# The second MLP in two passes: chunk 0 by plain products, chunks 1 and 2 together by seven block products

## The chip, the cores and the metric

The kernel runs as one program on one core of a Trainium2 chip. The metric is the device time of one execution in microseconds (us). A core has a matrix engine (TensorE: PE for its matmuls, PEld for the weight loads that run beside them), three engines for elementwise work (VectorE: DVE; ScalarE: ACT; GpSimd: POOL), and SyncE (SP), whose queue issues the transfers here. Every engine works through its own queue in order; an instruction that waits for a semaphore holds up all that stands behind it on that engine. Matmuls write to PSUM banks; everything else named here lies in SBUF or, for the inputs and outputs, in DRAM.

## The reference

The reference computes one step of a two-layer network on 1152 tokens (1024 latent, 128 context) of width 1024. Layer 0 is windowed attention and an MLP, layer 1 is a bidirectional state-space scan with a gated linear unit (GLU) and an MLP; then a final norm. The change concerns the MLP of layer 1 alone:

```
def _mlp(h, w1, w2):                 # h: tokens x 1024, w1: 1024 x 4096, w2: 4096 x 1024
    a = jax.nn.relu(h @ w1)
    return (a * a) @ w2
...
x = x + gate * _mlp(modulate(rmsnorm(x), shift, scale), w1, w2)
y = rmsnorm(x, final_norm_g)
```

## The kernel before

The 1152 tokens lie with the features on the partitions, as three chunks of 384 tokens: `x[0]`, `x[1]`, `x[2]`, each of 8 feature tiles of 128 (KT). Chunk 2 holds 256 latent and 128 context tokens, which have different modulation, so elementwise work on it is done in two pieces, 256 and 128 wide. Each float32 operand of a matmul is split into a high part (a rounded copy) and a low part (the rest), and each product takes three matmuls, `mm3`: high with high, high with low, low with high (L45 to L47). A split of a weight tile is one cast on ACT (L51) and one subtraction on DVE (L52), and it reads a raw tile that a DMA of 512 KB has filled.

`mlp(layer)` runs for both layers. It goes over 16 feature blocks `fb` of 256 hidden features. For each block there is a **first product** (for each chunk and each half m of the block: 8 x 3 matmuls of 384 columns into one PSUM bank, then relu and square on ACT and a split into `at`), and a **second product** (for each chunk and each of 8 output tiles: 2 x 3 matmuls, then `add_x`, which adds the gated bank to `x` on DVE). A block is thus 3 x 48 matmuls of the first product and then 3 x 48 of the second, 288 in all, and the MLP 16 x 288 = 4608.

What the steps of the prediction touch:

- `load` makes the weights of a block, w1 or w2: two raw halves of 128 x 1024, and of each a high and a low part. The raw tiles (`wr`, tag `wr`) have two buffers for everything, so the transfer of a raw half can be issued only when the subtraction that reads the half two places before it is done. The split w1 (tag `wq`, one buffer for the high part, one for the low) and the split w2 (tag `w2`, the same) exist once each: w1 of the next block can be written only when the first product of this block has ended, and w2 only when its second product has ended.
- In the block's code w2 is loaded ahead of the first product, and w1 of the next block between the first and the second product.
- `norm_stats` makes the row statistics of a chunk (`rb`), `norm_apply` the modulated input `mh`. In the second MLP `mh` of chunk 0 is there from the GLU, those of chunks 1 and 2 are made at the start.
- In the last block each chunk's second product is followed by `norm_stats` and `final`, which scales `x` and writes `y`.

The order of the work on each engine is set by a scheduler: the code is recorded in program order, and instructions whose inputs and buffers would be ready are moved up.

## Time and profile before

| | us |
|---|---|
| median of 3 runs (2797.89 to 2807.26) | 2802.87 |
| the profiled execution | 2799.74 |
| its span, first to last instruction | 2797.8 |
| second MLP, from its first matmul (1955.58) to the end of the span | 842.2 |
| PE busy / DVE busy / ACT busy / POOL busy in the span | 2609.5 / 1824.4 / 1096.1 / 366.6 |

The page gives busy time of each engine, then the span in 40 slices of 70 us (a digit is a share in tenths; PEclk is the clock granted to TensorE, in tenths of 2.4 GHz). Matmuls overlap in the pipeline, so their listed duration (0.34 us) is longer than the distance between their starts; where it matters the starts are compared. In the timeline a row gives start, duration, engine, line, operation, tiles, and in brackets the idle time before it and what ended it; rows of a kind that follow each other are merged with their count.

### The profile page before, as it was taken

Reading aid. Unit: us, or ns where it says so; the run is one execution under the profiler, and the core shown is the slowest. Engines: PE = TensorE matmul, PEld = TensorE weight load, DVE = VectorE, ACT = ScalarE, POOL = GpSimd, SP = SyncE. Lnnn points to the kernel's source line nnn. Section 1 sums busy time; section 2 is a strip of 40 time slices with the busy share of each in tenths; the row PEclk is TensorE's granted clock in tenths of the full one; section 3 lists DMA queues with packets and bytes.
Section 4 is the critical chain, followed back from the end, with each engine's and each line's share of the span. In section 5 each row is a group of like instructions: output and inputs, shape, how many; then the busy total and the mean of one; then the engine's idle time right before and its main releaser. Section 6 shows DMA issues by size and latency. Waiting matters only on the chain. (4 is left out here: it accounts for less than half of the span.)

```text
span 2797.8 us, 44016 instructions
## 1 busy us (share of the span) xinstructions
PE 2609.5 (93%) x16561; PEld 2462.1 (88%) x16561; DVE 1824.4 (65%) x4342; ACT 1096.1 (39%) x2295; POOL 366.6 (13%) x476
## 2 busy tenths in 40 slices
PE   6889999998899999999899687999999999999997
PEld 4767987886699989899899676999999999999997
DVE  4847777785576787887875799545645354454455
ACT  3545666662223323332333655434422222212224
POOL 1222222210022132121220400000000000000002
PEclk8999999999999999999999799999999999999998
DMA  7353222235532233132223586433110111111101
GB/s 264 109 169 105 84 79 74 81 116 189 180 103 75 70 95 90 55 105 71 88 83 91 174 251 180 141 121 113 46 46 31 46 46 46 34 43 46 46 31 68
DMA packets 128452, 271.67 MB, mean 97 GB/s; under 512 B 13296, under 2 KB 67952, under 8 KB 126832
## 3 DMA queue, kind: packets, MB, share of 16 engines
q1 hardware_dynamic: 128240, 268.86, 30.3%
q8 instruction: 131, 2.15, 0.3%
q14 instruction: 81, 0.66, 0.1%
HBM read 214.22 MB, written 39.81 MB: 91 GB/s over the span
## 5 line engine op out<-in xcount | busy, mean ns | idle before, releaser
L455 DVE SCALAR_TENSOR_TENSOR x<-m,mod,x 128x384 f32<-128x384 f32 (+2 forms) x1024 | 496.2, 512 | 149.2 <-PE m L47 145.3
L47 PE MATMUL m<-at,w 128*128 128x384 f32 x1536 | 523.4, 341 | 0.0
L45 PE MATMUL m<-at,w 128*128 128x384 f32 x1536 | 522.7, 340 | 0.8 <-DVE x L455 0.8
L46 PE MATMUL m<-at,w 128*128 128x384 f32 x1536 | 521.7, 340 | 0.0
L45 PE MATMUL m<-mh,w 128*128 128x384 f32 x1024 | 349.1, 342 | 1.9 <-ACT mh L237 1.9
L47 PE MATMUL m<-mh,w 128*128 128x384 f32 x1024 | 349.9, 342 | 0.0
L46 PE MATMUL m<-mh,w 128*128 128x384 f32 x1024 | 349.8, 342 | 0.0
L52 DVE TENSOR_TENSOR at<-r,at 128x384 fp32r<-128x384 f32 x192 | 111.6, 583 | 361.4 <-ACT at L51 361.2
L51 ACT CAST w<-wr 128x1024 fp32r<-128x1024 f32 x128 | 131.0, 1046 | 524.4 <-PE m L46 515.7
L47 PEld LDWEIGHTS m<-at,w 128*128 128x128 f32 x1536 | 289.1, 188 | 9.2 <-issue 8.9
L45 PEld LDWEIGHTS m<-at,w 128*128 128x128 f32 x1536 | 289.2, 188 | 3.8 <-issue 1.8
L46 PEld LDWEIGHTS m<-at,w 128*128 128x128 f32 x1536 | 289.1, 188 | 2.8 <-issue 2.5
L683 ACT ACTIVATE r<-m 128x384 f32<-128x384 f32 x192 | 93.8, 490 | 373.1 <-PE m L47 370.3
L45 PEld LDWEIGHTS m<-mh,w 128*128 128x128 f32 x1024 | 193.9, 190 | 7.4 <-issue 4.8
L52 DVE TENSOR_TENSOR w<-wr,w 128x1024 fp32r<-128x1024 f32 x128 | 156.6, 1243 | 64.9 <-ACT w L51 60.6
L47 PEld LDWEIGHTS m<-mh,w 128*128 128x128 f32 x1024 | 194.5, 190 | 3.6 <-issue 3.5
L46 PEld LDWEIGHTS m<-mh,w 128*128 128x128 f32 x1024 | 194.4, 190 | 1.6 <-issue 0.8
L45 PE MATMUL m<-h,w 128*128 128x384 f32 x512 | 174.4, 341 | 1.5 <-ACT w L51 0.7
L47 PE MATMUL m<-h,w 128*128 128x384 f32 x512 | 173.9, 340 | 1.2 <-DVE w L52 1.2
L46 PE MATMUL m<-h,w 128*128 128x384 f32 x512 | 174.5, 341 | 0.0
L1242 POOL TENSOR_TENSOR fo<-fo,rb 128x384 f32<-128x384 f32 x18 | 20.6, 1176 | 1034.7 <-ACT rb L224 1026.9
L389 POOL TENSOR_SCALAR pt<-pt,sst 128x512 f32<-128x512 f32 (+1 forms) x144 | 102.6, 724 | 298.4 <-DVE sst L387 153.8
(328 smaller groups left out, 5161.1 us busy)
## 6 DMA issues: line engine op xcount, KB each, us to landing
wr<-in_w_dram SPq DMA_DIRECT2D x128, 512.0 KB, 4.4
wm<-in_w_mod_dram SPq DMA_DIRECT2D x80, 512.0 KB, 4.6
wr<-in_glu_dram SPq DMA_DIRECT2D x48, 512.0 KB, 3.3
wr<-in_w_qo_dram SPq DMA_DIRECT2D x24, 512.0 KB, 3.3
wr<-in_w_qo_dram SPq DMA_DIRECT2D x48, 256.0 KB, 2.8
bt<-bt_d SPq DMA_DIRECT2D x16, 768.0 KB, 5.5
dt_d<-d SPq DMA_DIRECT2D x32, 294.0 KB, 2.1
D<-dt_d SPq DMA_DIRECT2D x16, 588.0 KB, 4.7
```

The source lines that it names most:

```text
L45: mm(out, lh, rh, start=first, stop=False)
L46: mm(out, lh, rl, start=False, stop=False)
L47: mm(out, ll, rh, start=False, stop=last)
L51: (ceng.copy if ceng is self.nc.scalar else ceng.tensor_copy)(h, src)
L52: seng.tensor_tensor(out=l, in0=src, in1=h, op=ALU.subtract)
L389: nc.gpsimd.tensor_scalar(p[:, e, :nk], p[:, e, :nk], rc[:, e:e + 1], 1.0, op0=ALU.mult, op1=ALU.mult)
L455: nc.vector.scalar_tensor_tensor(out=self.x[c][:, m, lo:hi], in0=ps[:, lo:hi], scalar=self.gate(layer, j, m, s), in1=self.x[c][:, m, lo:hi ...
L683: nc.scalar.activation(r, pt[:, :CW], AF.Relu)
L1242: nc.gpsimd.tensor_tensor(out=z, in0=z, in1=self.rb[c], op=ALU.mult)
```

## The change

`run` calls a new function `mlp1` for the second MLP; `mlp` stays for the first one.

**Pass A, chunk 0.** 16 blocks, first product 48 matmuls, second product 48. The first product of block fb + 1 stands ahead of the second product of block fb. w2 of block fb and w1 of block fb + 1 are loaded ahead of both. Beside it `h_seven` makes five combinations of the inputs of chunks 1 and 2 (sums on POOL, splits on ACT and DVE).

**Pass B, chunks 1 and 2.** 16 blocks again, so w1 and w2 are read a second time. The first product takes the 256 features as two halves of 128, the 1024 inputs as two halves of 512 and the two chunks as a 2 x 2 block product, in Winograd's form of Strassen's algorithm: seven products (`seven`) of 4 x 3 = 12 matmuls, 84 in place of 8 x 12 = 96. They accumulate in three banks `pa`, `pb`, `pc`; after a product a bank's partial sum is copied out (`keep`) or added to a kept one (`done`), then relu, square and split as before. The weights enter as seven tiles, some of them sums of quarters (`w_seven`: 4 sums and 7 subtractions on DVE, 7 casts on ACT, each 128 x 512); for the next block they are made during the second product, and `issue_after` keeps them behind the last square and split in the queues. `h_rest` makes the two inputs that are no sums, at the end of pass A. The second product is as before, 96 matmuls. `final0` writes chunk 0's output in blocks 1 and 2 of pass B, through one buffer `z`.

```diff
+    def w_half(self, fb, q, raw=None):
+        raw = self.R.tile([128, 1024], F32, name="wr", tag="wr", bufs=2)
+        self.nc.sync.dma_start(raw, self.a["w1"][1, fb][:, 1024 * q:1024 * q + 1024])
+        return raw.rearrange("p (k m c) -> p m k c", m=2, c=128)
+    def w_seven(self, fb, w, first=False):
+        nc, M, R = self.nc, self.M, self.R
+        r0, r1 = self.w_half(fb, 0), self.w_half(fb, 1)
+        a11, a21, a12, a22 = r0[:, 0], r0[:, 1], r1[:, 0], r1[:, 1]
...
+        def put(i, src, t):
+            nc.scalar.copy(t[:, 0], src)
+            nc.vector.tensor_tensor(out=t[:, 1], in0=src, in1=t[:, 0], op=ALU.subtract)
+            w[i] = t
+        def sx(x, y, op):
+            t = M.tile([128, 4, 128], F32, name="sx", tag="sx", bufs=2)
+            nc.vector.tensor_tensor(out=t, in0=x, in1=y, op=op)
+            return t
+        def single():
+            put(7, sx(a11, a21, ALU.subtract), one(R, "wo", 2))
+            yield
+            put(2, a12, one(R, "wo", 2))
+            yield
+            put(4, a22, one(M, "wz", 1))
+            yield
+        yield
+        if first:
+            yield from single()
+        t1, t5 = two("ws", "wq")
+        put(1, a11, t1)
+        yield
+        s1 = sx(a21, a22, ALU.add)
+        put(5, s1, t5)
+        yield
+        s2 = sx(s1, a11, ALU.subtract)
+        t6, t3 = two("ws", "wq")
+        put(6, s2, t6)
+        yield
+        put(3, sx(a12, s2, ALU.subtract), t3)
+        yield
+        if not first:
+            yield from single()
+    def seven(self, w, B, pa, pb, pc, evict):
+        for i in (1, 5, 6, 3, 7, 2, 4):
+            p = pa if i in (1, 6, 7, 4) else pb if i in (5, 3) else pc
+            for j in range(4):
...
+                for k, (x, y) in enumerate(((0, 0), (0, 1), (1, 0))):
+                    self.nc.tensor.matmul(p[:, :CW], w[i][:, x, j, :], B[i][j][y], start=f and k == 0,
+                                          stop=j == 3 and k == 2, skip_group_check=True)
...
+            evict(i)
+    def h_seven(self, B):
...
+        for j in range(4):
...
+            c, d = (M.tile([128, CW], F32, name="cd", tag="sx", bufs=2) for _ in range(2))
+            put = lambda i, src: self.split(B[i][j][0], B[i][j][1], src, nc.scalar, nc.vector)
+            self.h_part(1, j, a)
+            self.h_part(2, j, b)
+            yield
+            put(1, a)
+            gp.tensor_tensor(out=a, in0=b, in1=a, op=ALU.subtract)
+            put(5, a)
+            yield
+            self.h_part(2, j + 4, c)
+            self.h_part(1, j + 4, d)
+            yield
+            gp.tensor_tensor(out=b, in0=c, in1=b, op=ALU.subtract)
+            put(7, b)
+            yield
+            gp.tensor_tensor(out=c, in0=c, in1=a, op=ALU.subtract)
+            put(6, c)
+            gp.tensor_tensor(out=d, in0=d, in1=c, op=ALU.subtract)
+            put(4, d)
+            yield
+    def h_rest(self, B):
...
+    def mlp1(self):
...
+            def load(name, pool, tag, src):
+                w = [pool.tile([128, 2048], F32R, name=name, tag=tag, bufs=2) for _ in range(2)]
+                for q in range(2):
+                    sl = slice(1024 * q, 1024 * q + 1024)
+                    raw = self.R.tile([128, 1024], F32, name="wr", tag="wr", bufs=2)
+                    nc.sync.dma_start(raw, src[:, sl])
+                    self.split(w[0][:, sl], w[1][:, sl], raw, nc.scalar, nc.vector)
+                return w
...
+            def act(z, src):
+                at = M.tile([128, 2, CW], F32R, name="at", tag="at", bufs=4)
+                nc.scalar.activation(z, src, AF.Relu)
+                nc.scalar.activation(z, z, AF.Square)
+                self.last = (nc.scalar.copy(at[:, 0], z),
+                             nc.vector.tensor_tensor(out=at[:, 1], in0=z, in1=at[:, 0], op=ALU.subtract))
+                return at
...
+            w1 = load("w1", self.R, "wq", a["w1"][1, 0])
+            h = self.mh[0]
+            def fill():
+                yield from self.norm_stats(2)
+                yield from self.h_seven(B)
...
+            def first(w):
...
+            acts = first(w1)
+            for fb in range(nb):
+                w2 = load("w2", M, "w2", a["w2"][1, fb])
+                if fb + 1 < nb:
+                    w1 = load("w1", self.R, "wq", a["w1"][1, fb + 1])
+                    nxt = first(w1)
+                    next(gen, None)
+                    second(0, w2, acts)
+                    next(gen, None)
+                    acts = nxt
+                else:
+                    for _ in gen:
+                        pass
+                    ws = {}
+                    rest = self.h_rest(B)
+                    sums = self.w_seven(0, ws, True)
+                    def step(m):
+                        next(sums, None)
+                        next(rest, None)
+                    second(0, w2, acts, step)
+                    for _ in chain(sums, rest):
+                        pass
+            out = chain(self.norm_stats(0, 2), self.final0())
+            for fb in range(nb):
+                w2 = load("w2", M, "w2", a["w2"][1, fb])
+                pa, pb, pc = (ps.tile([128, 512], F32, name="m1", tag="acc") for _ in range(3))
...
+                def keep(i, p):
+                    z[i] = self.tt("r")
+                    nc.scalar.copy(z[i], p[:, :CW])
+                def done(o, i, p):
+                    nc.vector.tensor_tensor(out=z[i], in0=z[i], in1=p[:, :CW], op=ALU.add)
+                    at[o] = act(z[i], z[i])
...
+                self.seven(ws, B, pa, pb, pc, evict)
+                last = fb == nb - 1
+                wn = {}
+                sums = iter(()) if last else self.w_seven(fb + 1, wn)
+                sa, va = (i.ins for i in self.last)
+                def part():
+                    with tc.issue_after(sa), tc.issue_after(va):
+                        next(sums, None)
+                part()
+                for c in (2, 1):
+                    stats = self.norm_stats(c, 1) if last else iter(())
+                    def step(m):
+                        next(stats, None)
+                        part()
+                        if m % 2 and fb:
+                            next(out, None)
+                    second(c, w2, [at[0, c], at[1, c]], step)
+                    for _ in stats:
+                        pass
+                    if last:
+                        out = self.final(c, c == 1)
+                ws = wn
             for _ in out:
                 pass
-            for _ in gen:
-                pass
+    def final0(self):
+        nc = self.nc
+        for kt in range(KT):
+            z = self.M.tile([128, CW], F32, name="z", tag="z", bufs=1)
+            nc.scalar.activation(z, self.x[0][:, kt, :], AF.Copy, scale=self.gn[:, 4, kt:kt + 1])
+            nc.gpsimd.tensor_tensor(out=z, in0=z, in1=self.rb[0], op=ALU.mult)
+            nc.sync.dma_start(self.o["y"][0, :, kt], z)
+            yield
...
-        self.mlp(1)
+        self.mlp1()
```

Three places in the order of the built program. A number behind a name tells buffers of one name apart; `h_19343` is the input of chunk 0, `w1` and `w2` are split weights, `wr` raw halves, `m1` and `m2` the banks of the first and second product. Rows of the changed kernel have its own line numbers.

**PE, end of one block of the first loop and start of the next.** Before, the last matmuls of a block's second product and the first of the next block's first product:

```order
L45 MATMUL m2_21289<-at_21027,w2_20895 128x384
L46 MATMUL m2_21289<-at_21027,w2_20895 128x384
L47 MATMUL m2_21289<-at_21027,w2_20896 128x384
L45 MATMUL m1_21309<-h_19343,w1_21088 128x384
L46 MATMUL m1_21309<-h_19343,w1_21088 128x384
L47 MATMUL m1_21309<-h_19343,w1_21089 128x384
```

Now, in pass A, the end of block 11's second product and the start of block 13's first:

```order
L45 MATMUL m2_21944<-at_21713,w2_21798 128x384
L46 MATMUL m2_21944<-at_21713,w2_21798 128x384
L47 MATMUL m2_21944<-at_21713,w2_21799 128x384
L45 MATMUL m1_21975<-h_19343,w1_21965 128x384
L46 MATMUL m1_21975<-h_19343,w1_21965 128x384
L45 MATMUL m1_22006<-h_19343,w1_21965 128x384
L47 MATMUL m1_21975<-h_19343,w1_21966 128x384
```

The first product still follows the second directly, with three matmuls on the high part of w1 (`w1_21965`) moved ahead of the first on its low part (`w1_21966`).

**ACT, around the same place.** Before, from the last half of a block into the next (`L51 CAST` is the high part of a split):

```order
L51 CAST w1_20685<-wr_20687 128x1024
L683 ACTIVATE r_20680<-m1_20655 128x384
L51 CAST w1_20685<-wr_20691 128x1024
L684 ACTIVATE r_20680<-r_20680 128x384
L51 CAST at_20624<-r_20680 128x384
L51 CAST w2_20895<-wr_20897 128x1024
L51 CAST w2_20895<-wr_20901 128x1024
L683 ACTIVATE r_20931<-m1_20906 128x384
```

Now, the same block of pass A as above:

```order
L51 CAST hs11_20514<-cd_21720 128x384
L51 CAST w2_21955<-wr_21957 128x1024
L51 CAST w2_21955<-wr_21961 128x1024
L51 CAST w1_21965<-wr_21967 128x1024
L51 CAST w1_21965<-wr_21971 128x1024
L861 ACTIVATE r_22000<-m1_21975 128x384
```

The casts of w1 moved from the middle of the block before, ahead of the casts of w2, to right behind the casts of w2 of the same turn; on DVE the four subtractions stand in the same sequence, and on SP the transfers of `wr_21967` and `wr_21971` stand behind those of `wr_21957` and `wr_21961`.

**DVE, the second product of a block.** Before, chunk 2 (`x2`, two pieces a tile; `L455` is `add_x`):

```order
L455 SCALAR_TENSOR_TENSOR x2_72<-m2_21244,mod1_94,x2_72 128x256
L455 SCALAR_TENSOR_TENSOR x2_72<-m2_21244,mod1_94,x2_72 128x128
L455 SCALAR_TENSOR_TENSOR x2_72<-m2_21253,mod1_94,x2_72 128x256
L455 SCALAR_TENSOR_TENSOR x2_72<-m2_21253,mod1_94,x2_72 128x128
L455 SCALAR_TENSOR_TENSOR x2_72<-m2_21262,mod1_94,x2_72 128x256
L455 SCALAR_TENSOR_TENSOR x2_72<-m2_21262,mod1_94,x2_72 128x128
```

Now, pass B, a block in the middle (`ws` the seven weight tiles, `sx` sums of quarters):

```order
L455 SCALAR_TENSOR_TENSOR x2_72<-m2_24249,mod1_94,x2_72 128x256
L455 SCALAR_TENSOR_TENSOR x2_72<-m2_24249,mod1_94,x2_72 128x128
L726 TENSOR_TENSOR ws_24233<-sx_24245,ws_24233 128x512
L731 TENSOR_TENSOR sx_24258<-sx_24245,wr_24220 128x512
L455 SCALAR_TENSOR_TENSOR x2_72<-m2_24263,mod1_94,x2_72 128x256
L455 SCALAR_TENSOR_TENSOR x2_72<-m2_24263,mod1_94,x2_72 128x128
L726 TENSOR_TENSOR ws_24260<-sx_24258,ws_24260 128x512
L731 TENSOR_TENSOR sx_24272<-wr_24222,sx_24258 128x512
L455 SCALAR_TENSOR_TENSOR x2_72<-m2_24276,mod1_94,x2_72 128x256
```

Between the additions of chunk 2's eight tiles the eleven instructions on the next block's weights are now queued.

## Rows read from the trace of the kernel before

**Rows 1.** The page: busy time of the engines, and granted clock by slice.
```profile
PE 2609.5 (93%) x16561; PEld 2462.1 (88%) x16561; DVE 1824.4 (65%) x4342; ACT 1096.1 (39%) x2295; POOL 366.6 (13%) x476
PEclk8999999999999999999999799999999999999998
```
**Rows 2.** Second MLP by stage: us; busy PE, PEld, DVE, ACT, POOL; PEclk; DMA share; GB/s.
```profile
1955.58:1981.50 25.92, 23.43 (x128) 22.66 (x129) 21.66 (x52) 14.74 (x30) 0.00 (x0) 0.93 0.13 42
1981.50:2748.00 766.50, 766.50 (x4356) 766.03 (x4355) 357.14 (x652) 203.56 (x354) 0.00 (x0) 1.00 0.12 41
```
**Rows 3.** Timeline, where one block of the second MLP gives way to the next.
```profile
2114.48 0.34 PE L45 MATMUL m<-h,w 128*128 128x384 f32 x1
2114.50 2.00 ACT L51 CAST w<-wr 128x1024 fp32r<-128x1024 f32 x2 [21.99 <-PE m L46]
...
2115.59 2.36 DVE L52 TENSOR_TENSOR w<-wr,w 128x1024 fp32r<-128x1024 f32 x2 [0.16 <-ACT w L51]
...
2116.84 1.46 SPq L658 DMA_DIRECT2D wr<-in_w_dram  x2
```
**Rows 4.** Timeline, PE at the start of the second MLP.
```profile
1974.99 0.51 PE L223 MATMUL nrb<-ident,nst 128*128 128x128 f32 x3 [0.57 <-DVE nst L220]
1977.42 0.79 PE L45 MATMUL m<-mh,w 128*128 128x384 f32 x2 [1.92 <-ACT mh L237]
...
1980.64 0.52 PE L46 MATMUL m<-mh,w 128*128 128x384 f32 x1
```
**Rows 5.** DMA issues of that place: first, second; then all of L658 (to landing).
```profile
wr<-in_w_dram SPq DMA_DIRECT2D x1, 512.0 KB, 3.8
...
wr<-in_w_dram SPq DMA_DIRECT2D x1, 512.0 KB, 5.4
...
DMA to landing us min/median/max: 3.6/4.5/5.4
```
**Rows 6.** Timeline, SP and ACT: a cast of w1 that waits for its transfer.
```profile
1940.74 0.33 SPq L658 DMA_DIRECT2D wr<-in_w_dram  x1
...
1944.47 1.05 ACT L51 CAST w<-wr 128x1024 fp32r<-128x1024 f32 x1 [2.35 <-DMA wr<-in_w_dram]
```
**Rows 7.** Groups by form, second MLP: DVE, then POOL (count, busy us, mean ns).
```profile
L455 DVE SCALAR_TENSOR_TENSOR x<-m,mod,x 128x384 f32<-128x384 f32 x256 | 152.9, 615 | 68.6 <-PE m L47 68.4
L52 DVE TENSOR_TENSOR w<-wr,w 128x1024 fp32r<-128x1024 f32 x62 | 74.4, 1221 | 43.7 <-ACT w L51 43.6
L455 DVE SCALAR_TENSOR_TENSOR x<-m,mod,x 128x256 f32<-128x256 f32 x128 | 61.9, 483 | 40.3 <-PE m L47 40.2
L52 DVE TENSOR_TENSOR at<-r,at 128x384 fp32r<-128x384 f32 x96 | 53.3, 557 | 260.2 <-ACT at L51 260.2
L455 DVE SCALAR_TENSOR_TENSOR x<-m,mod,x 128x128 f32<-128x128 f32 x128 | 43.7, 342 | 0.0
...
L1242 POOL TENSOR_TENSOR fo<-fo,rb 128x384 f32<-128x384 f32 x18 | 20.6, 1176 | 1034.7 <-ACT rb L224 1026.9 <-ACT fo L1241 4.3 <-issue 3.5
```
**Rows 8.** Timeline, PE in the GLU: matmuls right behind a wait and later.
```profile
1755.57 0.78 PE L45 MATMUL gp<-ys,gw 128*128 128x384 f32 x2 [3.49 <-ACT ys L51]
...
1758.57 0.52 PE L46 MATMUL gp<-ys,gw 128*128 128x384 f32 x1
1758.89 0.52 PE L47 MATMUL gp<-ys,gw 128*128 128x384 f32 x1
...
1759.42 0.34 PE L46 MATMUL gp<-ys,gw 128*128 128x384 f32 x1
```
**Rows 9.** Windows behind another wait, in the first MLP (columns as in rows 2).
```profile
1176.00:1178.00 2.00, 1.02 (x17) 0.67 (x17) 1.94 (x11) 0.00 (x0) 0.00 (x0) 0.50 0.11 33
...
1182.00:1184.00 2.00, 2.00 (x12) 2.00 (x11) 2.00 (x5) 0.24 (x1) 1.29 (x2) 0.90 0.39 131
```
**Rows 10.** Group by form, whole kernel, DVE: a subtraction 512 wide.
```profile
L52 DVE TENSOR_TENSOR wo<-wr,wo 128x512 fp32r<-128x512 f32 x48 | 34.5, 720 | 6.9 <-ACT wo L51 6.6
```
**Rows 11.** Issues of the outputs in the last 47 us (KB each, us to landing).
```profile
out_y_dram<-fo SPq DMA_DIRECT2D x12, 384.0 KB, 2.3
```

More of the change, by code (lines that the diff above doesn't have):

```diff
@@ L698, in mlp @@
                         next(stats, None)
-                        if m % 2:
-                            next(out, None)
                     fill(1)
@@ L703, in mlp, with two, one @@
                         pass
-                    if fb == nb - 1 and layer == 1:
-                        out = self.final(c)
+            for _ in gen:
[8 more added lines that the diff above has]
+        a11, a21, a12, a22 = r0[:, 0], r0[:, 1], r1[:, 0], r1[:, 1]
+        def two(name, tag):
+            t = R.tile([128, 2, 2, 4, 128], F32R, name=name, tag=tag, bufs=2)
+            return t[:, 0], t[:, 1]
+        def one(pool, tag, bufs):
+            return pool.tile([128, 2, 4, 128], F32R, name="ws", tag=tag, bufs=bufs)
+        def put(i, src, t):
[30 more added lines that the diff above has]
+            yield from single()
@@ new lines, in h_part @@
+    def h_part(self, c, kt, out):
+        nc = self.nc
+        t = self.tt("nt")
+        for lo, hi, s in self.pieces(c):
+            nc.vector.scalar_tensor_tensor(out=t[:, lo:hi], in0=self.x[c][:, kt, lo:hi],
+                                           scalar=self.gs[1][1][:, kt, s:s + 1],
+                                           in1=self.rb[c][:, lo:hi], op0=ALU.mult, op1=ALU.mult)
+            nc.scalar.activation(out[:, lo:hi], t[:, lo:hi], AF.Identity, bias=self.shift(1, 1, kt, s))
```

88 lines of the change are left out of this document (83 added, 5 removed).

## The prediction

> **What bounds the kernel now.** I read the page first: PE is busy 93% of the span and the granted clock is near full in nearly every slice [rows 1]. Then the stage that the change touches, by windows: from 1981.5 to 2748 PE is busy for all of 766.5 us, at a granted clock of 1.00 (2.4 GHz), and starts 4356 matmuls, so one takes 766.5 / 4356 = 0.176 us and none waits [rows 2]. DVE is busy 47% there, ACT 27%, the DMA engines 12%. So in this stage time is the count of matmuls times 0.176 us, as long as PE never waits. Last I read one place, the change from one block to the next [rows 3]. The cast of the new w2 waits 22 us for the old one's last matmul and begins at 2114.50; the first subtraction follows at 2115.59; the transfer of the next raw half is issued at 2116.84. PE doesn't notice: at 2114.48 it goes on with a first product of 144 matmuls (25.3 us) whose weights were ready. The single buffers of w1, w2 and two raw halves cost nothing because 144 matmuls cover each refill. That is what to see: the chain exists, and its cover is long.
>
> **What is saved.** Pass B has 84 + 96 matmuls a block, pass A 48 + 48, together 276 where 288 were: 16 x 12 = 192 fewer, and 192 x 0.176 = **-33.8 us**. The start of the second MLP loses its wait for chunk 2's input: 0.57 and 1.92 us of idle, then some ten matmuls at about 0.32 us instead of 0.176 (until past 1980.64), 1.4 us [rows 4]: **-3.9 us**. The statistics on PE stay, elsewhere.
>
> **What pass A adds.** Now the first product of one block stands directly behind the second product of another, and it needs a w1 that can't be there. In the order on ACT, DVE and SP, w2's split and then w1's transfers and split are queued in this place. Both raw buffers hold w2's halves until DVE has subtracted them, and w2's split waits for PE's last matmul. So PE itself starts the chain on which it then waits. By the same chain before, with PE's next matmul due at 2114.48:
>
> - ACT casts w2's first half, DVE subtracts it, SP issues w1's first half at 2116.84: 2.36 us [rows 3].
> - The transfer lands 3.8 us after issue, as the first of a pair did here; the second took 5.4, and the extremes are 3.6 and 5.4 [rows 5].
> - ACT casts w1's half: 1.05 us, and it starts as soon as the data lands (issue 1940.74, cast 1944.47, 3.73 apart) [rows 6].
>
> 2.36 + 3.8 + 0.03 + 1.05 and a few hundredths to PE are 7.3 us of idle. Then three matmuls can run on the high part; the low part needs 1.22 us of DVE [rows 7] from the cast's end, so PE goes on at 8.5 us having done 0.5 us of work: 8.0 us lost.
>
> The clock comes on top. In the GLU a wait of 3.49 us was followed by matmuls whose starts are 0.32 us apart (1758.57, 1758.89), the clock of 1.2 GHz, until about 1759.2, 3.7 us after PE went on [rows 8]. Behind a 7.3 us wait I expect the same. From 8.5 to 11.0 us that makes 8 matmuls where 14 would run: another 1.1 us. If the clock stayed full, w1's second half would bind instead (issued 1.13 us later, 5.4 to land, then cast and subtraction: 11.1 us), for about 0.5 us. So a turn costs 8.5 to 9.1 us, and I take **9.1**. If half clock lasts 6 us, as behind the wait that ended near 1176.5 (0.50, and still 0.90 at 1182 to 1184) [rows 9], it is 10.2.
>
> There are 14 such turns: the first products of blocks 2 to 15. 14 x 9.1 = **+127.4 us** (8.3 to 10.2 each: 116 to 143). Block 1's first product waits only for cast and subtraction, since its transfer can land during block 0's; and the last second product waits for one cast of w2: together **+2.4**.
>
> By the Trainium skill (DMA: Bandwidth & Descriptors, Anatomy of one DMA) a transfer costs about 2.0 us fixed plus its bytes at 436 GB/s, an estimate of 3.2 us for 512 KB, and the turns together would cost 8 us less. The trace has 3.6 to 3.8, and I keep that. The Trainium skill's first page (Trainium Kernel Development and Optimization, Best Practices) asks for double buffers so that transfers overlap compute; it speaks against pass A, but it would blame the kernel before as well, where the trace shows no wait at all.
>
> **Beside PE in pass A.** `h_seven` adds 16 sums to POOL at 1.18 us [rows 7] and 44 half-microsecond instructions each to DVE and ACT, spread over ten turns of 26 us in which DVE has 4 x 1.22 + 8 x 0.62 + 2 x 0.56 = 11 us of other work [rows 7]. They stand in the second product, ahead of the chain, and end before it: nothing. The 64 more transfers of 512 KB find the DMA engines at 12%: nothing outside the turns.
>
> **From A to B.** The last second product (8.4 us) and the first products of pass B lie beside DVE's work on `h_rest` (16 x 0.41 + 8 x 0.62 = 11.5), 11 subtractions and sums 512 wide at 0.72 [rows 10] (7.9), 8 additions (4.9) and w2 (2.4): 26.7, or some 24 if queued instructions overlap by 0.08 each (two of 1.22 take 2.36 [rows 3]). PE needs the last of it for its fifth product, after about 8.4 + 60 x 0.176 = 19 us, and starts 1 us late behind a cast: **+6** (2 to 12).
>
> **Pass B.** ACT is at 13 of 32 us a block. DVE: PE's 84 first matmuls end at 14.8 us of a block and the first tile of the second product at 15.9; from there DVE has 8 x (0.483 + 0.342) for chunk 2, 11 x 0.72 for the weights and one split, 15.1 us. Six banks rotate, so chunk 1's sixth tile, due at 28.5 us, needs chunk 2's last addition. At listed durations that is done at 31.0; with the overlap at 28.7. Lost a block: 0 to 2.5 us. The queue is dense, so I stay near the overlap, with a little for subtractions that wait for a cast: 0.6, and 15 x 0.6 = **+9** (0 to 37). `issue_after` holds the sums behind the last split, on which nothing of PE's next 40 matmuls waits. `final0`'s eight tiles go through one buffer: cast 0.6, POOL 1.18 and a transfer of half the 384 KB that land in 2.3 [rows 11] make 4 us against 2.1 of spacing, and ACT's queue stands meanwhile: **+4** (0 to 16). The tail is as before.
>
> **Sum:** -33.8 - 3.9 + 127.4 + 2.4 + 6 + 9 + 4 = +111.1. On the profiled execution's 2799.74 that is 2910.8, so **2911 us**. The median of before is 2802.87, 3.1 higher, less than its runs differ; I leave the number.
>
> **Rivals.**
>
> - *Faster: pass A's turns cost PE nothing.* The point is (33.8 + 3.9 - 2.4 - 6 - 9 - 4) / 14 = 1.2 us a turn; below it the change gains, and with no wait at all the time is 2911 - 127 = 2784. It would need PE to run other matmuls in the turn. For it: PE's order does move three matmuls up. Against: these three read w1's high part, and all else behind them is behind that wait. 0.03.
> - *Only the transfer is hidden* (w1's raw halves in time): w2's two casts, then w1's, 3.2 us, and the low part, some 3.9 a turn: 2838. Against: both raw buffers are full at that point. 0.03.
> - *DVE binds pass B* at listed durations: 2.5 in place of 0.6 a block, +28: 2939. For it: 11 more instructions in a queue that PE's banks wait on. Against: the overlap in [rows 3]. 0.14.
> - *Half clock lasts longer*, 10.2 a turn: 2926. For it: [rows 9]. Against: [rows 4, 8]. 0.12.
> - *Shorter turns*: full clock, or 3.6 us to land: 8.3 a turn, 2900. 0.08.
> - That the products aren't fewer is out: 84 stand in the order.
>
> **How the numbers follow.** The forecast has 0.60. Lowest sum with the turns in place: -37.7 + 116 + 2 + 2 = +82, 2882. Highest: turns of 10.2 and pass B at its worst, the rest as taken: -37.7 + 143 + 2.4 + 6 + 37 + 4 = +155, 2955. The range is 2880 to 2955; outside it lie the first two rivals. A measurement of this kernel tells about 0.3% (8 us) from no change. Faster by more: 0.03, the first rival; within: 0.02, some way between the first two; slower: 0.95.
>
> **What would show it.** In pass A: 14 gaps of about 7 us on PE, ended by a cast of w1 which itself waited for its transfer; granted clock 0.5 behind each; a turn of some 26 us for 96 matmuls, where 16.9 would do. In pass B: PE busy throughout, 180 matmuls in about 32 us. I am wrong if PE's gaps in pass A are under 2 us, or if pass B takes over 34 us a block.

## The result, and the profile after

The changed kernel takes 2918.98 us (median of 4 runs, 2914.43 to 2921.07), the one before 2802.48 us beside it (4 runs, 2797.89 to 2807.26): a ratio of 1.0412, 95% interval 1.0397 to 1.0426, so 116 us slower. The forecast was 2911, its range 2880 to 2955. The profiled execution took 2914.43 us with a span of 2912.6, 114.8 us more than the span of before.

The head of the page after, which answers to [rows 1]. The columns and slices are as there.

```profile
PE 2615.3 (90%) x16369; PEld 2446.5 (84%) x16369; DVE 1994.9 (68%) x4618; ACT 1231.9 (42%) x2519; POOL 384.2 (13%) x492
...
PE   6889999988899999999996879997777889999997
PEclk8999999999999999999998999998888899999998
```

PE is busy 6 us longer than before and the span is 115 us longer: PE does fewer matmuls, does some of them at half clock, and stands idle. The slices show where: from the 28th to the 32nd, 1966 to 2330 us, PE is busy 7 or 8 tenths and the clock is at 8. That is pass A; the slices of pass B behind it are at 9 up to the tail.

Then the waits of PE through the whole second MLP: who waited, for whom, us in total, times, longest.

```profile
PE m L45 <- ACT w L51: 97.6, 16, 7.5
PE m L45 <- DVE x L455: 8.4, 17, 1.2
PE nrb L223 <- DVE nst L220: 3.3, 1, 3.3
PE m L769 <- DVE ws L726: 1.4, 1, 1.4
```

One line carries nearly all of it: 16 waits for a cast of a split weight, 97.6 us, 13 of them 6.9 to 7.5 us long. One of them, as the timeline shows it (the answer to [rows 3], where the same chain stood beside a first product of 144 matmuls):

```profile
2114.28 0.34 PE L47 MATMUL m<-at,w 128*128 128x384 f32 x1
2114.48 1.99 ACT L51 CAST w<-wr 128x1024 fp32r<-128x1024 f32 x2 [2.85 <-PE m L46]
...
2115.55 2.36 DVE L52 TENSOR_TENSOR w<-wr,w 128x1024 fp32r<-128x1024 f32 x2 [0.28 <-ACT w L51]
2116.80 6.63 SPq L854 DMA_DIRECT2D wr<-in_w_dram  x3
2120.77 1.04 ACT L51 CAST w<-wr 128x1024 fp32r<-128x1024 f32 x1 [4.31 <-DMA wr<-in_w_dram]
...
2121.87 0.69 PE L45 MATMUL m<-h,w 128*128 128x384 f32 x1 [7.25 <-ACT w L51]
...
2122.35 0.52 PE L46 MATMUL m<-h,w 128*128 128x384 f32 x1
...
2122.67 0.52 PE L45 MATMUL m<-h,w 128*128 128x384 f32 x1
...
2123.13 0.69 PE L47 MATMUL m<-h,w 128*128 128x384 f32 x1
2123.27 1.04 ACT L51 CAST w<-wr 128x1024 fp32r<-128x1024 f32 x1 [1.45 <-DMA wr<-in_w_dram]
```

PE's last matmul of the second product starts at 2114.28. ACT casts w2, which that product has just released (2114.48), DVE subtracts it (2115.55), SP issues w1's transfer (2116.80, 2.32 us after the cast began), the data lands and ACT casts it (2120.77, 3.97 later), PE goes on (2121.87, 1.10 later). The bracket on PE's row gives 7.25 us of idle. After it the starts are 0.32 us apart, and the low part comes at 2123.13.

The clock around it, and the stages, by windows (length, busy time and count of PE, PEld, DVE, ACT, POOL, then the granted clock and DMA): first the wait, what follows it, and the rest of this turn; then all 14 turns; then pass B's block 0, blocks 1 and 2, blocks 3 to 14, and block 15.

```profile
2114.62:2121.87 7.25, 0.00 (x0) 0.00 (x1) 3.00 (x4) 2.89 (x3) 0.00 (x0) 0.85 0.40 136
2121.87:2126.18 4.31, 4.31 (x13) 3.87 (x14) 2.43 (x2) 1.04 (x1) 0.00 (x0) 0.50 0.39 138
2126.18:2141.13 14.95, 14.95 (x85) 14.63 (x84) 7.84 (x15) 5.85 (x13) 3.24 (x3) 0.99 0.11 36
1981.18:2358.61 377.43, 278.45 (x1360) 268.13 (x1359) 175.45 (x260) 122.98 (x197) 17.07 (x16) 0.82 0.23 78
2368.01:2405.48 37.47, 33.71 (x182) 30.86 (x181) 33.03 (x63) 17.25 (x32) 0.00 (x0) 1.00 0.24 85
2405.48:2474.38 68.90, 65.97 (x377) 64.10 (x376) 49.55 (x100) 34.27 (x65) 8.29 (x7) 1.00 0.24 78
2474.38:2861.18 386.80, 382.03 (x2162) 375.47 (x2161) 270.08 (x529) 163.45 (x289) 1.03 (x1) 1.00 0.20 67
2861.18:2894.27 33.09, 33.09 (x196) 32.79 (x195) 21.41 (x48) 21.12 (x41) 1.32 (x2) 1.00 0.00 1
```

Behind the wait PE has a clock of 0.50 for 4.31 us, then 0.99. The 14 turns take 377.43 us, 26.96 each, of which 96 matmuls at 0.176 are 16.9: **10.06 us a turn are lost, 140.9 in all**. Blocks 3 to 14 take 386.80 / 12 = 32.23 us.

### The profile page after: what moved, and what is told of

Same layout as the page of the kernel before. It is cut to its first block, busy times and chain, and to the rows that moved or that the text cites. A ratio compares the mean times of both kernels' runs of the same rounds, so it can differ in the third digit from the quotient of the medians.

```text
span 2912.6 us, 43999 instructions
## 1 busy us (share of the span) xinstructions
PE 2615.3 (90%) x16369; PEld 2446.5 (84%) x16369; DVE 1994.9 (68%) x4618; ACT 1231.9 (42%) x2519; POOL 384.2 (13%) x492
## 5 line engine op out<-in xcount | busy, mean ns | idle before, releaser
L455 DVE SCALAR_TENSOR_TENSOR x<-m,mod,x 128x384 f32<-128x384 f32 (+2 forms) x1024 | 488.3, 512 | 90.6 <-PE m L47 86.6
L51 ACT CAST w<-wr 128x1024 fp32r<-128x1024 f32 x160 | 162.9, 1045 | 376.7 <-PE m L46 292.9
L45 PEld LDWEIGHTS m<-at,w 128*128 128x128 f32 x1536 | 288.7, 188 | 22.5 <-PE m L47 11.9
L45 PE MATMUL m<-h,w 128*128 128x384 f32 x512 | 192.8, 377 | 97.9 <-ACT w L51 97.2
L52 DVE TENSOR_TENSOR w<-wr,w 128x1024 fp32r<-128x1024 f32 x160 | 194.8, 1240 | 102.0 <-ACT w L51 97.6
L45 PEld LDWEIGHTS m<-h,w 128*128 128x128 f32 x512 | 109.0, 213 | 104.9 <-ACT w L51 102.4
L47 PE MATMUL m<-h,w 128*128 128x384 f32 x512 | 187.7, 367 | 2.7 <-DVE w L52 2.7
L46 PE MATMUL m<-h,w 128*128 128x384 f32 x512 | 187.4, 366 | 0.0
L45 PE MATMUL m<-mh,w 128*128 128x384 f32 x512 | 176.8, 345 | 0.0
L47 PE MATMUL m<-mh,w 128*128 128x384 f32 x512 | 176.8, 346 | 0.0
L46 PE MATMUL m<-mh,w 128*128 128x384 f32 x512 | 176.4, 344 | 0.0
L52 DVE TENSOR_TENSOR at<-r,at 128x384 fp32r<-128x384 f32 x96 | 59.0, 616 | 101.2 <-ACT at L51 101.0
L682 ACT ACTIVATE r<-m 128x384 f32<-128x384 f32 x96 | 47.1, 491 | 173.8 <-PE m L47 173.5
L864 DVE TENSOR_TENSOR at<-r,at 128x384 fp32r<-128x384 f32 x80 | 44.5, 556 | 108.1 <-ACT at L863 108.1
L377 ACT ACTIVATE pt<-sps,sst 128x512 f32<-128x512 f32 (+1 forms) x144 | 89.4, 626 | 67.8 <-DVE sst L366 67.5
L47 PEld LDWEIGHTS m<-h,w 128*128 128x128 f32 x512 | 105.8, 207 | 10.8 <-DVE w L52 9.0
```

What stands on the lines that cost most here:

```text
L45: mm(out, lh, rh, start=first, stop=False)
L46: mm(out, lh, rl, start=False, stop=False)
L47: mm(out, ll, rh, start=False, stop=last)
L51: (ceng.copy if ceng is self.nc.scalar else ceng.tensor_copy)(h, src)
L52: seng.tensor_tensor(out=l, in0=src, in1=h, op=ALU.subtract)
L377: nc.scalar.activation(p[:, e, :nk], sps[e][:, :nk], AF.Exp, scale=SCALE, bias=ng[:, e:e + 1], accum_out=sm[:, e:e + 1])
```

## The experiments

All times are medians. Where a kernel had one run only, stages are compared, not totals: the code ahead of the second MLP is the same in the change and the eleven kernels made from it, yet the stage's first matmul starts anywhere from 1952.7 to 1962.1 us. A pass whose code is the same repeats better, though not always to a tenth: pass A of the change took 413.87 us (1954.14 to 2368.01) and 413.96 in a run that left it as it was, pass A with exchanged loads 275.5 to 277.0 us in seven kernels, and pass B of the change 526.0 to 527.4 us in the four kernels that share it.

### The order of the two loads

```diff
             for fb in range(nb):
-                w2 = load("w2", M, "w2", a["w2"][1, fb])
                 if fb + 1 < nb:
                     w1 = load("w1", self.R, "wq", a["w1"][1, fb + 1])
+                w2 = load("w2", M, "w2", a["w2"][1, fb])
+                if fb + 1 < nb:
                     nxt = first(w1)
```

> Pass A with w1 of block fb+1 loaded ahead of w2 of block fb, where the change has w2 first; nothing else differs. My theory: the 10.06 us that a turn loses (2116 to 2358 in the trace of the change: 26.96 us a turn, 96 matmuls at 0.176 are 16.9) come from a chain that PE itself starts: last use of w2, cast, subtraction, w1's transfer, cast. With w1 first, its raw buffers come free when w2 of the block before is subtracted, one first product (8.4 us) earlier, and its casts and subtractions can run beside the second product; w2's transfer then has a whole first product to land. The 14 gaps fall from 7.2 us to under 0.5, the clock stays at 1.00 there, and the time is 2919 - 14 x 10 = 2779 us. Rival, the transfer is hidden but casts and subtractions of both weights stay in the turn (queued on ACT and DVE behind work that follows PE): 3.9 us a turn stay, 2833. Rival, the gaps come from the number of transfers and not from their order: no change, 2919.

Measured: 2777.82 us (2777.02 to 2781.93), a ratio of 0.9914 (0.9886 to 0.9942) to the kernel before. Of the change that is 141 us less, and 26 us under before. The waits of PE in the second MLP, and pass A and pass B by windows:

```profile
PE m L45 <- DVE x L455: 8.2, 17, 1.2
PE m L45 <- ACT w L51: 1.9, 2, 1.0
PE m L47 <- DVE w L52: 1.5, 3, 0.8
```

```profile
1956.06:2231.51 275.45, 272.02 (x1555) 269.95 (x1555) 191.03 (x299) 137.73 (x227) 20.49 (x16) 1.00 0.36 119
2231.51:2757.54 526.03, 515.19 (x2911) 503.21 (x2910) 373.40 (x737) 235.51 (x426) 10.61 (x10) 1.00 0.20 66
```

The 97.6 us behind casts are 1.9, pass A runs at a clock of 1.00 and takes 275.45 us where 1536 matmuls at 0.176 are 270.3. The same bytes move through the same buffers by the same instructions (DMA share 0.36 in pass A, in place of 0.23, as the same transfers fall into less time). So the order made the gaps: with the same number of transfers, the same bandwidth and the same single buffers they are gone, and both rivals fall. Whether a second buffer for each weight would have closed them in the old order as well, no run shows. Pass B takes 526.03 us, in the change 526.26: the exchange leaves it as it was.

### What the clock costs

```diff
                     second(0, w2, acts)
                     next(gen, None)
                     acts = nxt
+                    if fb + 2 < nb:
+                        pt = ps.tile([128, 512], F32, name="fil", tag="acc")
+                        for k in range(40):
+                            nc.tensor.matmul(pt[:, :CW], h[k % 8][0][:, :128], h[k % 8][0],
+                                             start=True, stop=True)
```

> The change, with 40 matmuls of the chunk's own input (their output is read by nobody) put on PE in each of the 14 turns, between the second product and the next first product: 40 x 0.176 = 7.0 us, about the length of the gap. They take no weights that are waited for. It prices the clock by itself. My theory: a turn's 10.06 us are 7.2 us of idle and 2.9 us behind it, most of it half clock (some 17 matmuls 0.32 us apart in place of 0.176). With the filler the clock stays at 1.00, and behind it PE is bound by w1's second half, which comes 11.1 us after the first cast of w2: some 8.7 to 9.0 us a turn are left, so 14 x 1.0 to 1.4 = 14 to 19 us less, 2900 to 2905. Rival, the 2.9 us are all the chain of w1's low parts and second half and the clock hides behind it: no change, 2919. Rival, the filler itself delays the first product, since it ends later than the weights come: 2920 to 2930.

Measured: 2889.75 us (ratio 1.0307, 1.0283 to 1.0332), 29 us under the change. More than the 14 to 19 that I expected: 2.1 us a turn. The scheduler had also moved six matmuls that don't need w1's low part ahead of the first that does, where the change has three. So a second run with half the filler (`range(20)`), in which eight are moved up:

> The change with 20 matmuls of filler in each of pass A's 14 turns where the run before had 40: 3.5 us of the wait are covered and some 3.6 us of idle are left. With a filler eight matmuls that need high parts alone stand ahead of the first low part (six with 40 of filler, three without), so the run with 40 changed two things. If the clock is what the filler gave back: behind 3.6 us of idle PE is at half clock again (in the GLU of before, 3.49 us were enough), and the gain is at most the five matmuls moved up, 14 x 0.9 = 12 us: 2907 to 2919. If the moved matmuls gave it: as with 40 or more, 2885 to 2890.

Measured: 2908.89 us (1.0371, 1.0354 to 1.0388), 10 us under the change. Windows, first with 40 of filler (most of a filler; then one whole turn, from its first product through the next filler), then with 20 (the idle behind a filler; what follows; the rest of the turn with the next filler and the next idle):

```profile
2109.80:2116.51 6.71, 6.40 (x37) 6.08 (x36) 2.50 (x4) 2.38 (x3) 0.00 (x0) 1.00 0.47 150
2116.51:2140.96 24.45, 24.22 (x136) 23.54 (x136) 13.53 (x21) 9.80 (x16) 3.62 (x3) 1.00 0.26 87
```

```profile
2121.50:2125.04 3.54, 0.00 (x1) 0.01 (x1) 0.03 (x1) 1.04 (x1) 0.00 (x0) 0.97 0.74 268
2125.04:2128.34 3.30, 3.30 (x10) 3.30 (x11) 2.32 (x2) 1.04 (x1) 0.00 (x0) 0.51 0.33 104
2128.34:2150.65 22.31, 18.68 (x107) 18.36 (x106) 11.20 (x20) 8.75 (x15) 3.29 (x3) 1.00 0.24 78
```

With 40 the clock is 1.00 all through; with 20, 3.54 us of idle are left and the clock behind them is 0.51 for 3.30 us. Pass A takes 380.89 us with 40, 403.28 with 20, 413.87 with none. The 22.4 us between the two fillers, 1.6 us a turn, can't be the moved matmuls, since the run with fewer moved is the faster; they are the clock. The 10.6 us between 20 and none, 0.76 a turn, go to the matmuls that were moved up into time in which PE waited for low parts (five at 0.176 are 0.9), and to a half clock that lasted somewhat shorter; which of the two has how much wasn't separated.

The rows also say why 40 gave more than expected. PE around the filler, where the change has 2114.28, 2121.87 and 2123.13:

```profile
2108.93 0.33 PE L47 MATMUL m<-at,w 128*128 128x384 f32 x1
...
2116.51 0.44 PE L45 MATMUL m<-h,w 128*128 128x384 f32 x1 [0.31 <-ACT w L51]
...
2117.77 0.44 PE L47 MATMUL m<-h,w 128*128 128x384 f32 x1
```

The first product and its first low part come as late as in the change (7.58 and 8.84 us after the last matmul of the second product, there 7.59 and 8.85). Of the 8.84 us, seven paces of 0.176 are work, six of them the matmuls moved up; 7.6 us are lost by then. The whole turn takes 24.45 us, 7.6 over 16.9. So at full clock nothing more is lost behind the first low part, and w1's second half, which I expected to hold PE there, doesn't. In the change 8.1 us are lost by the first low part (8.85 less four paces), and 10.06 in a turn: the difference, some 1.9 us a turn, is an estimate of what the half clock costs.

### The size of the chain's links

```diff
-                    nc.sync.dma_start(raw, src[:, sl])
-                    self.split(w[0][:, sl], w[1][:, sl], raw, nc.scalar, nc.vector)
+                    for u in (0, 512):
+                        su = slice(1024 * q + u, 1024 * q + u + 512)
+                        nc.sync.dma_start(raw[:, u:u + 512], src[:, su])
+                    for u in (0, 512):
+                        su = slice(1024 * q + u, 1024 * q + u + 512)
+                        self.split(w[0][:, su], w[1][:, su], raw[:, u:u + 512], nc.scalar, nc.vector)
```

> The change, with every transfer, cast and subtraction of pass A's and pass B's w2 and pass A's w1 cut in two: pieces of 128x512, 256 KB a transfer, in the same buffers and the same order. It changes the size of every link of the chain and leaves its order. My theory, link by link: two casts of w2's first half overlap its two subtractions (raw half free after some 2.0 us where it was 2.36), a transfer of 256 KB lands in 2.6 to 2.9 us where 512 KB took 3.8 to 4.0, the first cast of w1 takes 0.57 where it took 1.05: a gap of about 5.4 us where it was 7.2, half clock behind it as before: 14 x 1.8 = 25 us less, 2894. Rival, the landing is set by what else the queue moves and not by its size: only the casts shrink, 6.4 us, 14 x 0.8, 2908. Rival, the doubled number of transfers and instructions costs more than it gives in pass A and pass B: 2919 or over.

Measured: 2892.51 us (1.032, 1.0296 to 1.0345), 26 us under the change. A turn in its timeline:

```profile
2107.52 0.34 PE L47 MATMUL m<-at,w 128*128 128x384 f32 x1
2107.72 2.18 ACT L51 CAST w<-wr 128x512 fp32r<-128x512 f32 x4 [2.85 <-PE m L46]
...
2108.43 2.49 DVE L52 TENSOR_TENSOR w<-wr,w 128x512 fp32r<-128x512 f32 x4
2109.74 6.22 SPq L856 DMA_DIRECT2D wr<-in_w_dram  x6
2113.12 1.28 ACT L51 CAST w<-wr 128x512 fp32r<-128x512 f32 x2 [3.23 <-DMA wr<-in_w_dram]
2113.77 2.79 DVE L52 TENSOR_TENSOR w<-wr,w 128x512 fp32r<-128x512 f32 x4 [2.85 <-ACT w L51]
...
2113.79 0.69 PE L45 MATMUL m<-h,w 128*128 128x384 f32 x1 [5.94 <-ACT w L51]
```

Cast to issue is 2.02 us (2.32 in the change), issue to cast 3.38 (3.97), cast to PE 0.67 (1.10): every link shrank, and the idle is 5.94 us here. The transfer shrank least, 0.6 us for half the bytes, so the idle fell by 1.3 us where I expected 1.8. The total came out as expected all the same, since pass A got 27.8 us shorter (386.07 in place of 413.87), 2.0 a turn, more than the idle alone: behind the wait the low part now comes after half as much subtraction, and half clock lasts shorter (in the mean 11 starts a turn at about 0.32, in the change 13). The price is paid in block 0 of pass B, 43.3 us in place of 37.5, so the first expectation was right in its sum and not in its parts.

### Pass B: the sums and the output tiles

The first run of these leaves work out: the sums of block 0 serve all blocks.

```diff
-                sums = iter(()) if last else self.w_seven(fb + 1, wn)
+                wn = ws
+                sums = iter(())
```

> Pass B of the change uses the weights' sums of block 0 in all blocks: the transfers of w1, the sums, casts and subtractions of blocks 1 to 15 are left out (11 DVE and 7 ACT instructions of 128x512 and two transfers a block). Pass A is as in the change. It shows what the sums cost PE. My theory: in pass B DVE's queue is late by 0.4 us at one tile of chunk 1 in every block, since the sums stand between chunk 2's additions; without them no bank is waited for, a block takes 31.7 us in place of 32.23, and the time falls by 15 x 0.5 = 8 us; the blocks with final0's tiles (34.45 us each) also lose part of their extra 2.2 us. 2908 to 2911. Rival, the 0.4 us are the additions' own pace and the sums cost nothing: 2919. Rival, the sums also hold PE's first product by their ACT casts, unseen in the waits: a block of 31.3, 2905.

Measured: 2897.16 us (one run). Blocks 2 to 14 of pass B by a window:

```profile
2436.11:2843.88 407.77, 407.77 (x2342) 407.77 (x2342) 218.05 (x429) 128.15 (x228) 7.12 (x7) 1.00 0.11 38
```

A block takes 31.37 us (407.77 / 13, PE busy for all of it), 0.86 less than 32.23, so the sums cost more than the 0.5 I expected. In the change the starts of a block's matmuls show the waits: at the fifth and sixth tile of chunk 1 four matmuls start 0.57, 0.08, 0.13 and 0.08 us later than the pace, together 0.86. The list of waits has 0.4 of it. The third theory, with unseen casts, had forecast nearly this number (31.3 and 2905), but not the place: the seven products take 14.73 us in a block with the sums and without them, and what goes lies in the second product. What the sums cost is the late bank and the starts behind it. The blocks with output tiles fell to 33.26 and 31.37 us, from 34.47 and 34.43. Pass A was not touched (413.96 us). Between the profiled executions the spans differ by 17.3 us; 16 of them are pass B and 1.4 lie ahead of the second MLP, where nothing was changed.

Then the same sums, spread over both chunks, on top of the exchanged loads:

```diff
                         next(stats, None)
-                        part()
+                        if m % 2:
+                            part()
```

> As the one above with the sums spread over both chunks, but with chunk 0's output tiles where the change has them (four a chunk, blocks 1 and 2 of pass B). Theory: regular blocks 31.4 to 31.5 us; blocks 1 and 2 about 1 to 2 us longer: 2767. Rival, the sums' place does not matter, only their number: regular blocks stay at 32.23: 2778.

Measured: 2762.39 us (one run). Blocks 4 to 14 by a window:

```profile
2363.76:2708.78 345.02, 345.02 (x1981) 345.02 (x1981) 246.93 (x485) 149.80 (x264) 0.00 (x0) 1.00 0.20 68
```

345.02 / 11 = 31.37 us, PE busy throughout, with DVE busy for 22.4 us a block, in the change 270.08 / 12 = 22.5. So DVE was never short of time in pass B; the eleven instructions stood in the wrong place. Blocks 1 to 3, beside the output tiles, took 32.74, 31.70 and 33.98. ACT's timeline around the end of block 2, and the wait of PE that follows:

```profile
2328.90 0.62 ACT L984 ACTIVATE z<-x,gn 128x384 f32<-128x384 f32 x1 [2.60 <-DMA out_y_dram<-z]
2329.42 0.60 ACT L725 CAST ws<-sx 128x512 fp32r<-128x512 f32 x1
2329.93 0.62 ACT L725 CAST ws<-wr 128x512 fp32r<-128x512 f32 x1
2332.58 0.62 ACT L984 ACTIVATE z<-x,gn 128x384 f32<-128x384 f32 x1 [2.03 <-DMA out_y_dram<-z]
2335.01 1.04 ACT L51 CAST w<-wr 128x1024 fp32r<-128x1024 f32 x1 [1.81 <-DMA wr<-in_w_dram]
2335.96 0.86 ACT L930 COPY r<-m 128x384 f32<-128x384 f32 x2
2336.48 1.31 PE L769 MATMUL m<-ot,ws 128*128 128x384 f32 x6 [2.34 <-ACT r L930]
```

The casts of `z` (L984) stand 2.60 and 2.03 us until the output transfer has left the one buffer; w2's cast comes late behind them (2335.01), having waited 1.81 us more for a transfer that SP issued at 2331.08, behind those of the output; and the copies `r` (L930) that free PE's banks stand behind that cast. PE waited 2.34 us at 2336.48. Two edits address this. The first takes the output tiles at half the pace, one behind every fourth output tile:

```diff
-                        if m % 2 and fb:
+                        if m % 4 == 3 and fb:
                             next(out, None)
```

With the change's place of the sums:

> Pass A with w1 ahead of w2; chunk 0's output tiles one behind every fourth tile over four blocks of pass B; the sums where the change has them. Theory: the tiles' extra 2.2 us in each of two blocks (34.45 against 32.23) come from one buffer that is taken every 2.1 us and held for some 4; at a spacing of 4.2 us nothing waits for it, and blocks 1 to 4 take 32.2 to 32.4 us: 2778 - 4 = 2774. Rival, the tiles cost what their instructions cost on ACT, wherever they stand: 2778.

and with the sums spread:

> Pass A with w1 ahead of w2; in pass B one piece of the next weights' sums is queued behind every second tile of the second product, through both chunks, where the change queues one behind every tile and is done within chunk 2; the eight output tiles of chunk 0 go one behind every fourth tile, over four blocks in place of two. My theory: a block's 0.85 us of waits for banks (32.23 against 31.37 without the sums) come from eleven DVE instructions of 0.72 us squeezed between chunk 2's additions; spread, DVE keeps pace: blocks of 31.4 to 31.5, 14 x 0.8 = 11 us; the output tiles stop costing 2.2 us in each of two blocks, 4 us. 2778 - 15 = 2763 us. Rival: spread, the sums delay chunk 1's additions instead and PE's first product of the next block waits for its banks: 2778 to 2785. Rival: only the one of the two moves works: 2767 or 2774.

These two leave out part of the output: with this line in the last block too, two of the four pairs of chunk 2's output tiles are neither scaled nor written. Measured: 2780.5 us (one run) and 2763.84 us (0.9847, 0.9829 to 0.9865). With the whole output written (the old spacing in the last block):

> Pass A with w1 ahead of w2, the sums spread, one buffer for z, chunk 0's output tiles one behind every fourth tile over four blocks, the rest of the output as in the change. In the run like this that wrote part of chunk 2's output alone, the blocks beside the tiles took 34.06, 31.46 and 32.38 us: 3.8 us over 31.37 in all, hardly less than the 4.3 us at a spacing of 2.1. If one buffer is what costs, at any spacing under the 4 us that it is held: the same blocks again, 2762. If that run was an odd one: blocks of 31.4, 2758.

Measured: 2765.75 us (one run); blocks 1 to 4 took 31.37, 35.59, 31.37 and 32.32 us, 5.2 us over 31.37 together; the three blocks beside the tiles had lost 4.3 at the shorter spacing. Slower output tiles gained nothing, and not for the one buffer alone: of the 5.2 us, 4.2 are in block 2, where chunk 0's statistics now stand among the seven products. Behind their matmuls and a wait of 0.62 us the granted clock was 0.55 over 3.67 us. The second edit gives `z` a second buffer (`bufs=2` at both places):

> Pass A with w1 ahead of w2, the sums spread over both chunks, and two buffers in place of one for the tile z, through which chunk 0's output tiles and one squared relu of each block go. In the run with the sums spread alone, three blocks beside the output tiles lost 4.3 us together: ACT stood 2.0 to 2.6 us at a cast of z that waited for the transfer out of the one buffer, w2's transfer stood behind that output transfer on SP, and PE then waited 2.34 us for a bank whose copy was queued behind w2's cast. My theory: with two buffers a tile has 4.2 us until its buffer is wanted again, about what cast, product and transfer take, and ACT no longer stands: blocks 1 to 3 at 31.4 to 31.9 us, 2762 - 3.5 = 2758 to 2760. Rival: it is SP's queue, where output tiles stand ahead of w2's transfers: the blocks stay at 32.7, 31.7 and 34.0, 2762.

> As the one above, and with chunk 0's output tiles one behind every fourth tile of the second product over four blocks (the output of chunk 2 as in the change, all of it written). Theory: nothing waits for z in either; 2757 to 2760, not to be told from the one above. Rival: two buffers are too few at a spacing of 2.1 us and enough at 4.2: 1 to 3 us less than the one above.

Measured: 2764.45 us (0.9856, 0.9839 to 0.9872) with two buffers alone, 2767.58 (0.9866, 0.9851 to 0.9881) with the wide spacing as well. Both miss the forecast of 2757 to 2760, and the totals can't be told from the single run with the sums spread, 2762.39. By stages they can: pass B is 512.7 us there, 510.0 with two buffers, 512.2 with the wide spacing. With two buffers blocks 1 to 3 take 32.74, 31.70 and 31.37: the wait of 2.34 us is gone, and the 1.4 us in block 1 that stay are the statistics of chunk 0 on PE. With the wide spacing ACT still waits for `z` three times, 1.58 us at most, and PE doesn't notice; but block 2 takes 35.45 us, since the statistics stand among its seven products as with one buffer, with a wait of 0.62 us and a granted clock of 0.59 over 3.24 us behind them. What PE still waits for in pass B with two buffers alone, the three longest:

```profile
PE m L769 <- DVE ws L726: 1.2, 1, 1.2
PE m L769 <- DVE hr L836: 0.6, 1, 0.6
PE m L769 <- DVE r L933: 0.5, 1, 0.5
```

All of these are in block 0. Both kernels, with the exchanged loads, beat the one before by 1.3 to 1.5%.

## Why the prediction was right, and where it was off

The direction, the place and the chain of pass A were as put. That the sum came out 4 us from the measured one is in part luck: two terms were 13.5 and 7.8 us off, with opposite signs. The working as a ledger, in us: the stage from the first to the last matmul of the second MLP is 822.68 before and 939.96 after; 4608 and 4416 matmuls at 0.176 are 811.0 and 777.2 of it.

| term | predicted | measured |
|---|---|---|
| fewer products | -33.8 | -33.8, by count at the same pace |
| before's time without products that goes | -3.9 | -11.7 |
| 14 turns | +127.4 (9.1 each) | +140.9 (10.06 each) |
| first turn, last w2 | +2.4 | +2.7 |
| from A to B (block 0: 37.47 - 31.68) | +6 | +5.8 |
| pass B, 15 blocks (32.23 - 31.68 each) | +9 | +8.3, and 0.9 for statistics in block 15 |
| output tiles, blocks 1 and 2 | +4 | +4.4 |
| before and behind the stage | 0 | -2.4 |
| sum | +111.1 | +115.1 (spans: +114.8) |

**The turns.** The chain was right link by link: 2.32 us from cast to issue (2.36 in [rows 3]), 3.97 to land ([rows 5] gave 3.8), 1.10 to PE; the 13 waits of full length are 6.9 to 7.5 us, 7.2 in the mean, where 7.3 were forecast. **The step that failed is the next one, the clock behind the wait.** I took half clock to last 3.7 us after PE goes on, from the one wait in the GLU [rows 8], and 1.8 us for it and the low part together. The trace has 2.9: half clock lasted 4.3 to 5.9 us in 12 of the turns, 2.7 in one, and 5.0 behind the second wait of the turn that waits in two pieces; up to 18 starts at half pace. This counts to the last such start; by the same count [rows 8] has 3.3. That is nearer to [rows 9], which I had as the rival of 10.2 us a turn at 0.12 (I read 6 us from it; by this count it is 4.9, from 1176.98 to 1181.89); the turns went by that rival, and only the terms below kept the time near the forecast's. Two rows of one thing that lie apart called for a value between them at least, not for the smaller one. The runs with filler price the clock at 1.6 us a turn at least, and at some 1.9 by the rows at the first low part.

**The time that went with the old order.** I took off the 3.9 us that PE waits at the start [rows 4]; 7.8 more went, which I left in place with the words that the statistics stay elsewhere: they, and a wait of 1.25 us in the last block of before:

```profile
2769.60 0.80 PE L211 MATMUL nps<-ones,nacc 128*128 128x1 f32 x6 [1.25 <-DVE nacc L205]
```

After, chunk 2's statistics stand at 2008 to 2015 in a turn in which PE would have waited anyway (its wait for w1 is 2.30 us there and 3.30 for the statistics), and chunk 0's are part of the 4.4 us of the output tiles. A wait doesn't add to another one in the same gap. This and the clock are of opposite sign and cancel in part: +13.5 for the turns, -7.8 here.

**Pass B.** The forecast took 0.6 us a block between 0 and 2.5, and 0.55 over a pace of 0.176 was measured; against PE's own pace there (31.37 us) it is 0.86. The resource named, DVE's queue before PE's banks, was right, and so was the overlap of queued instructions [rows 3]: the rival at listed durations (2.5 a block) didn't come. "DVE binds" would have been the wrong name for it: spread over the block, the same instructions cost nothing.

**The landing.** The trace of the change has 3.5, 4.0 and 5.5 us (least, median, most) for its 56 transfers of 512 KB in the 14 turns, and a median of 3.2 for the 48 of 512 KB that load the GLU's weights. The formula of the Trainium skill (DMA: Bandwidth & Descriptors, Anatomy of one DMA), which that section fits for transfers issued from GpSimd while those here are issued from SP, would make it an estimate of 3.2 for 512 KB. The trace agrees for the GLU's weights and not for those of pass A, and there the measured one decides. In the run with 256 KB pieces, several of them in flight, the first data were there 3.38 us after issue. That formula would make it an estimate of 2.6.

**Double buffers.** The Trainium skill (Trainium Kernel Development and Optimization, Best Practices) asks for two buffers so that transfers overlap compute. No run here gives the split weights two. Pass A kept one buffer of each split weight, and the exchange of two loads removed all but 5 us of the 143.5 that pass A lost, without another byte of memory. What was missing was a whole product between the release of a buffer and the need for its next content, and the order gave that.

**The rival with pass A free of waits** would have been 2784 by the prediction's sum; the kernel with the loads exchanged has 2777.8. The turns were all that stood between the seven products and their gain.

## What to carry to other kernels

With single buffers, follow for each buffer who releases it and which product stands between that release and the next need; software pipelining that turns the order of products around must turn the order of their loads around too, or the last use of one weight starts the transfer of the very next one. Count the clock into every wait of some microseconds on the matrix engine, from the longest row that the trace has as well as from the shortest. Work for the next block belongs where the queue has room over the whole block, not where it is first possible: the same instructions cost 0.86 us a block or nothing.

## What the runs showed of the hardware that was not expected

- The half clock behind a wait was not of one length: after waits of 6.9 to 7.5 us it lasted from 2.7 to 5.9 us in pass A's turns, and behind the 3.54 us of idle shown with 20 of filler the granted clock was 0.51 for 3.30 us.
- It didn't take a wait of several microseconds: behind twelve matmuls of one column (chunk 0's statistics, 1.4 us) and 0.62 us of idle, in the two kernels with the wide spacing that write the whole output, the granted clock was 0.55 and 0.59 over the next 3 to 4 us.
- The pace of matmuls differs by product with nothing waiting: 0.1754 us in the seven products (84 in 14.73 us) and 0.1733 in the second product (96 in 16.64 us); the 0.176 of [rows 2] is the pace of before.
- A list of waits shows 0.39 to 0.42 us at the late bank of a block and not the smaller delays behind it; the distances of the starts show 0.86 us, and taking the sums away gave back 0.86.
- Totals of kernels that share all code ahead of a stage differ by up to 9 us at that stage's start, while passes of the second MLP whose code is the same differ by up to 1.5 us (275.5 to 277.0), and regular blocks of pass B by some 0.05. Effects of a few microseconds are read from stages.
